# Attention products of a two-block transformer: from two ticks of the weight stream into one, in a chain

## The chip, the core and the metric

The kernel runs on one core of a Trainium2 chip. The metric is the device time of one execution in microseconds (us); lower is better. A profiled execution gives the trace from which all rows here are taken.

## The reference

Two transformer blocks run one after the other on 256 positions of width 1024, each two layers deep. Both contain softmax attention over few positions and many wide products with weights that are used once. Cut to what matters:

```python
# first block, per layer: a mixer of three branches, then SwiGLU
proj = x @ w_in                      # a_q a_k a_v | b_h b_b b_c | c_q c_k c_v | g_a g_b g_c
y_a = sliding_window_attention(a_q, a_k, a_v, sinks, slopes)   # 8 heads of 64, window 128, 2 key heads
y_b = gated_short_conv(b_h, b_b, b_c, conv_w)
y_c = moba_attention(c_q, c_k, c_v, slopes)                    # 8 heads of 64; causal over 256 here
x = layer_norm(ALPHA * x + (sigmoid(g_a) * (y_a @ w_br_a) + sigmoid(g_b) * (y_b @ w_br_b)
                            + sigmoid(g_c) * (y_c @ w_br_c)) @ w_out)
x = layer_norm(ALPHA * x + swiglu(x))
# second block, per layer, on a latent stream h and a context stream hc:
#   half a SwiGLU; then a mixer; then half a SwiGLU, all gated by products of c with w_ada
attn = attend(q_lat, [k_ctx, k_lat], [v_ctx, v_lat])           # 8 heads of 64 + 32 rotated
h = h + gt2 * merge(u @ w_bgate, conv_module, attn @ w_o_mla, fourier_mix)
#   the context stream does the same with its own keys, in the first layer only
```

## The kernel before

All weights come from memory in 765 chunks of 512 KB. ACT copies each chunk into a high part `wh`, DVE subtracts for the low part `wl` (L261), and every product of the main loops is three matmuls of high and low parts (`mm3`, through `mm`, L373). A main matmul has 256 or 512 columns.

The main loops take the weights through `wtile()` or `wchunk()`. Each time a chunk is used up they call `tick()`. A tick first takes a job of the ada products if one is due (a DMA and two DVE products named `junk`, L547), and then advances every generator in `sides` by one `next()`. What a generator emits in that step is marked to be issued after the main loop's last matmul (`issue_after(self.last_mm.ins)`); the Tile scheduler then places each instruction on its engine by its own model of when the operands are ready, so an attention product may come some way behind the tick, between main matmuls. Each engine takes its instructions in order.

Attention runs in such generators. `attn1` serves both kinds of the first block, four pairs of heads each (kind 0 the sliding window, kind 1 the other); `attn2` serves the second block in eight steps, over 256 keys for the context stream (`nk` = 1) and 512 for the latent stream (`nk` = 2). A step `s` takes two ticks. In the first tick it emits the logits of pair `s` into two banks of tag "at" and their softmax, `turn(2s - 2)` (the transposes of the first head of pair `s - 1`, three in `attn1`, `2 * nk` in `attn2`), and the values products of pair `s - 2` into the bank "pv". In the second tick it emits `turn(2s - 1)`, the second head. `turn` puts its transposes into a PSUM bank of tag "st" (there is one) and ACT copies it to `pts`.

`softmax_step` for one head is a chain over two engines: DVE adds the distance term to the logits (`z`), takes two row maxima, scales them (`nb`); ACT takes the exponentials of two parts with their sums `sm`, and of the sink (`es`); DVE adds the sink's and takes 1/sum (`rc`); ACT multiplies `z` by `rc`, first 128 columns, then 256. The transposes read that `z`. The weight splits `wh` and `wl` and the ada products stand on the same two engines.

PSUM tags: "mm" has four banks (the main loops' results), "at" two, "st", "pv" and others one (`bank`). `finish(side)` runs a generator to its end.

Of the kernel before, what the change touches and what calls it, by code (L numbers as in the profile page):

```python
# [19 lines left out]
P = 128  # L20
D = 1024
KD = D // P
T = 256
# [202 lines left out]
class Weights:  # L226


    def __init__(self, kb, dram, ahead_split, ahead_load):
        self.kb, self.dram, self.n = kb, dram, dram.shape[0]  # L230
        self.loaded = self.split = self.pos = 0
        self.raw, self.parts = {}, {}
        self.ahead_split, self.ahead_load = ahead_split, ahead_load
        self.hold = None
# [45 lines left out]
class Kernel:  # L280
    NRAW, NSPLIT, NS, NADA, CPD = 6, 5, 45, 2, 1

    def __init__(self, tc, sb, ps, aps, vec_at):
        self.tc, self.nc, self.sb, self.ps = tc, tc.nc, sb, ps
        self.aps, self.vec_at = aps, vec_at
        self.n = 0
        self.sides = []
        self.last_root = None
        self.ticks = 0
        self.ada_jobs, self.ada_next = [], 0.0  # L290
        self.cur, self.cur_i = None, 8


    def act(self, out, in_, func, bias=0.0, scale=1.0, accum_out=None):
# [46 lines left out]
    def tick(self):  # L341
        self.ticks += 1
        if self.ada_jobs and self.ticks >= self.ada_next:
            self.ada_next += self.ada_jobs[0][1]
            self.ada_jobs.pop(0)[2]()
        with self.tc.issue_after(self.last_mm.ins):
            for s in list(self.sides):
                if next(s, "end") == "end":
                    self.sides.remove(s)

    def finish(self, side):
        if side in self.sides:
            self.sides.remove(side)
        for _ in side:
            pass

    def wtile(self):
        if self.cur_i == 8:
            if self.cur is not None:
                self.tick()  # L360
            self.cur, self.cur_i = self.w.get(), 0
        i = self.cur_i
        self.cur_i += 1
        return self.cur[0][:, i, :], self.cur[1][:, i, :]
# [5 lines left out]
        return self.cur  # L370

    def mm(self, out, a, b, start, stop):
        return self.nc.tensor.matmul(out, a, b, start=start, stop=stop)  # L373

    def mm3(self, out, a, b, start, stop):
        self.mm(out, a[0], b[0], start, False)
# [547 lines left out]
    def attn1(self, kind, l, heads, q, k, v, out):  # L924

        ps, pts = {}, {}
        n = len(heads) // 2

        def turn(i):
            z = ps.pop(i)
            pt = self.bank("st", "pt").rearrange("p a b -> p (a b)")[:, :384]
            for c in range(3):
                self.nc.tensor.transpose(pt[:, c * P:(c + 1) * P], z[:, c * P:(c + 1) * P], self.ident)
            t = self.slot("pts").rearrange("p a b -> p (a b)")[:, :384]
            self.act(t, pt, AF.Copy)
            pts[i] = t

        while self.ticks % 2 != kind:  # L940
            yield
        for s in range(n + 2):
            if s < n:
                pair = heads[2 * s:2 * s + 2]
                lgs = [self.bank("at", "lg").rearrange("p a b -> p (a b)")[:, :384] for _ in pair]
                for qa, ka in (((0, P), (0, P)), ((P, T), (0, T))):
                    for (h, qt, p0, kt, *_), lg in zip(pair, lgs):
                        o = lg[:, :P] if qa[0] == 0 else lg[:, P:]
                        self.mm(o, q[qt][p0:p0 + 64, qa[0]:qa[1]], k[kt][p0:p0 + 64, ka[0]:ka[1]], True, True)
                for j in range(2):  # L950
                    ps[2 * s + j] = self.softmax_step(kind, pair[j][0], lgs[j], 384, l)
            if 0 <= s - 1 < n:
                turn(2 * s - 2)
            if 0 <= s - 2 < n:
                pair = heads[2 * s - 4:2 * s - 2]
                ts = [pts.pop(2 * s - 4 + j) for j in range(2)]
                o = self.bank("pv", "pv")[:, 0, :]
                for (*_, vc, ot, op), t in zip(pair, ts):
                    self.mm(o[op:op + 64, :], v[0][:, vc:vc + 64], t[:, :T], True, False)
                for (*_, vc, ot, op), t in zip(pair, ts):  # L960
                    self.mm(o[op:op + 64, P:], v[1][:, vc:vc + 64], t[:, 2 * P:], False, True)
                self.split_into(out[0][ot // 2][:, ot % 2, :], out[1][ot // 2][:, ot % 2, :], o)
            yield
            if 0 <= s - 1 < n:
                turn(2 * s - 1)
            yield

    def mixer1(self, l, xs, xa):
# [327 lines left out]
    def attn2(self, q, keys, vals, out, first):  # L1296


        nk = len(keys)
        scale = 96.0 ** -0.5  # L1300
        n = 8
        ps, pts = {}, {}
        pv = None

        def turn(i):
            p = ps.pop(i)
            pt = self.bank("st", "pt2").rearrange("p a b -> p (a b)")[:, :nk * T]
            for c in range(2 * nk):
                self.nc.tensor.transpose(pt[:, c * P:(c + 1) * P], p[:, c * P:(c + 1) * P], self.ident)  # L1309
            t = self.slot("pts2").rearrange("p a b -> p (a b)")[:, :nk * T]  # L1310
            self.act(t, pt, AF.Copy)
            pts[i] = t

        for s in range(n + 2):
            hp, qb = divmod(s, 2)
            while s < n and len(q) < max(hp + 1, first):
                yield
            if s < n:
                lgs = [self.bank("at", "lg2") for _ in range(2)]
                for j in range(2):  # L1320
                    qa = q[hp][0:96, j, qb * P:(qb + 1) * P]
                    for c in range(nk):
                        self.mm(lgs[j][:, c, :], qa, keys[c][hp][0:96, j, :], True, True)
                for j in range(2):
                    lf = lgs[j].rearrange("p a b -> p (a b)")[:, :nk * T]
                    mx, nb, sm, rc = self.small("mx", 1), self.small("nb", 1), self.small("sm", 1), self.small("rc", 1)
                    self.nc.vector.tensor_reduce(mx, lf, AX.X, ALU.max)
                    self.ts(nb, mx, -scale, None, ALU.mult)
                    p = self.slot("p2").rearrange("p a b -> p (a b)")[:, :nk * T]
                    self.act(p, lf, AF.Exp, bias=nb, scale=scale, accum_out=sm)  # L1330
                    self.nc.vector.reciprocal(rc, sm)
                    self.act(p, p, AF.Copy, scale=rc)
                    ps[2 * s + j] = p
            if 0 <= s - 1 < n:
                turn(2 * s - 2)
            if 0 <= s - 2 < n:
                hp, qb = divmod(s - 2, 2)
                ts = [pts.pop(2 * s - 4 + j) for j in range(2)]
                if qb == 0:
                    pv = self.bank("pv", "pv2")[:, 0, :]  # L1340
                for c in range(2 * nk):
                    for j in range(2):
                        self.mm(pv[64 * j:64 * j + 64, qb * P:(qb + 1) * P],
                                vals[c][:, 64 * (2 * hp + j):64 * (2 * hp + j) + 64],
                                ts[j][:, c * P:(c + 1) * P], c == 0, c == 2 * nk - 1)
                if qb == 1:
                    self.split_into(out[0][hp // 2][:, hp % 2, :], out[1][hp // 2][:, hp % 2, :], pv)
            yield
            if 0 <= s - 1 < n:
                turn(2 * s - 1)  # L1350
            yield

    def conv_side(self, l, ready, out):
# [443 lines left out]
```

## Time and profile before

| what | value |
|---|---|
| runs | 2925.15, 2925.62, 2922.3 us; median 2925.15 us |
| profiled execution | 2921.71 us, of which the span of its trace is 2919.9 us |
| TensorE (PE) busy | 2882.8 us, 99% of the span |
| VectorE (DVE) busy | 2060.6 us, 71% |
| ScalarE (ACT) busy | 1336.2 us, 46% |
| mean granted clock of TensorE | 0.998 of full speed |

Read it so: PE is the engine whose work makes the time; the shares of DVE and ACT are means over stages that differ. In a timeline a row gives the start, the duration, the engine, the line, and the tile written and the tiles read; PE's durations overlap, so the distance between starts is what a matmul costs. An idle time stands in brackets with what ended it.

### The profile page before, as it was taken

What the parts mean: (1) busy time and instruction counts of PE and PEld (TensorE: products, weight loads), DVE (VectorE), ACT (ScalarE), POOL (GpSimd) and SP (SyncE); (2) the same over time, 40 slices, a digit from 0 to 9 for tenths busy, and PEclk for the clock granted to TensorE, in tenths of its full rate; (3) what the DMA queues carried; (4) which work ended last, traced back from release to release, by engine and by line L of the source; (5) the groups of instructions that cost most, each with busy time, mean ns of one, the idle gap of its engine ahead of it and who ended that gap; (6) DMA issues with size and microseconds to landing.
All of it is one profiled execution on the core that took longest, in us unless ns stands there. A gap on an engine that the chain in (4) does not pass through costs nothing. (4 is left out here: it accounts for less than half of the span.)

```text
span 2919.9 us, 51534 instructions
## 1 busy us (share of the span) xinstructions
PE 2882.8 (99%) x21000; PEld 2699.4 (92%) x21000; DVE 2060.6 (71%) x3506; ACT 1336.2 (46%) x2100; POOL 109.0 (4%) x121
## 2 busy tenths in 40 slices
PE   8999999999999999999999999999999999999999
PEld 7999999899999999999999998888888888899998
DVE  7879667648657787798888785555765556877655
ACT  6645445744444432256656642222322224665444
POOL 1001001000001000010010000000100001000000
PEclk9999999999999999999999999999999999999999
DMA  7665655454555764544553453433355543435453
GB/s 271 203 224 180 219 194 164 142 181 159 201 182 166 232 223 167 171 156 144 166 178 111 152 173 131 137 130 116 110 187 166 166 159 116 162 106 170 162 182 109
DMA packets 134589, 486.66 MB, mean 167 GB/s; under 512 B 14928, under 2 KB 15184, under 8 KB 134352
## 3 DMA queue, kind: packets, MB, share of 16 engines
q1 hardware_dynamic: 133776, 482.58, 49.8%
q8 instruction: 165, 2.70, 0.4%
q10 hardware_dynamic: 576, 0.79, 0.1%
q14 instruction: 72, 0.59, 0.1%
HBM read 482.26 MB, written 1.05 MB: 166 GB/s over the span
## 5 line engine op out<-in xcount | busy, mean ns | idle before, releaser
L302 ACT ACTIVATE wh<-raw 128x1024 fp32r<-128x1024 f32 x765 | 809.5, 1059 | 1243.9 <-issue 269.9
L261 DVE TENSOR_TENSOR wl<-raw,wh 128x1024 fp32r<-128x1024 f32 x765 | 939.5, 1230 | 511.3 <-ACT wh L302 505.6
L547 DVE SCALAR_TENSOR_TENSOR junk<-ada,cb 128x1024 bf16<-128x1024 f32 x256 | 313.3, 1224 | 4.3 <-DMA ada<-in_w_ada_dram 2.2
L373 PE MATMUL f<-xh,wh 128*128 128x256 f32 x704 | 198.8, 283 | 0.0
L373 PE MATMUL f<-xh,wl 128*128 128x256 f32 x704 | 198.4, 282 | 0.0
L373 PE MATMUL f<-xl,wh 128*128 128x256 f32 x704 | 198.1, 281 | 0.0
L373 PE MATMUL g<-xh,wh 128*128 128x256 f32 x608 | 173.7, 286 | 8.8 <-ACT wh L302 7.3
L373 PE MATMUL g<-xl,wh 128*128 128x256 f32 x608 | 173.0, 285 | 0.6 <-DVE xl L308 0.6
L373 PE MATMUL g<-xh,wl 128*128 128x256 f32 x608 | 173.0, 285 | 0.0
L373 PE MATMUL bg<-wh,wh 128*128 128x256 f32 x576 | 166.8, 290 | 0.8 <-DVE q L305 0.8
L373 PE MATMUL bg<-wh,wl 128*128 128x256 f32 x576 | 163.1, 283 | 0.0
L373 PE MATMUL bg<-wl,wh 128*128 128x256 f32 x576 | 162.5, 282 | 0.0
L373 PE MATMUL b<-uh,wl 128*128 128x512 f32 (+1 forms) x384 | 145.6, 380 | 0.0
L373 PE MATMUL a<-uh,wh 128*128 128x512 f32 (+1 forms) x384 | 145.4, 380 | 0.0
L373 PE MATMUL a<-wl,wh 128*128 128x256 f32 x512 | 144.7, 283 | 0.0
L373 PE MATMUL a<-wh,wl 128*128 128x256 f32 x512 | 144.7, 283 | 0.0
L373 PE MATMUL a<-uh,wl 128*128 128x512 f32 (+1 forms) x384 | 144.1, 375 | 0.0
L373 PE MATMUL b<-ul,wh 128*128 128x512 f32 (+1 forms) x384 | 144.0, 375 | 0.0
L373 PE MATMUL a<-wh,wh 128*128 128x256 f32 x512 | 143.7, 281 | 0.0
L373 PE MATMUL a<-ul,wh 128*128 128x512 f32 (+1 forms) x384 | 143.7, 374 | 0.0
L373 PE MATMUL b<-uh,wh 128*128 128x512 f32 (+1 forms) x384 | 143.6, 374 | 0.0
L1180 POOL TENSOR_TENSOR sq<-sq,sq 128x256 f32<-128x256 f32 x63 | 64.6, 1033 | 2105.0 <-ACT sq L302 2103.6
(429 smaller groups left out, 8685.4 us busy)
## 6 DMA issues: line engine op xcount, KB each, us to landing
raw<-in_w_dram SPq DMA_DIRECT2D x765, 512.0 KB, 3.3
ada<-in_w_ada_dram SPq DMA_DIRECT2D x144, 512.0 KB, 4.1
hc<-in_ctx_dram SPq DMA_DIRECT2D x8, 256.0 KB, 4.9
x<-in_x_dram SPq DMA_DIRECT2D x4, 256.0 KB, 6.4
out_dram<-out SPq DMA_DIRECT2D x4, 256.0 KB, 2.4
cb<-in_c_dram SPq DMA_DIRECT2D x1, 512.0 KB, 8.2
cb<-in_c_ctx_dram SPq DMA_DIRECT2D x1, 512.0 KB, 8.2
dft<-in_dft_dram ACTq DMA_DIRECT2D x2, 256.0 KB, 3.3
```

The costliest lines, as they stand in the source:

```text
L261: self.last_split = kb.nc.vector.tensor_tensor(lo.rearrange("p a b -> p (a b)"), raw, f.bitcast(F32), ALU.subtract)
L302: return self.nc.scalar.activation(out, in_, func, **kw)
L373: return self.nc.tensor.matmul(out, a, b, start=start, stop=stop)
L547: self.nc.vector.scalar_tensor_tensor(junk, raw, 1.0, self.cb[:, s, :], ALU.mult, ALU.mult, accum_out=self.mods[:, l, s, c:c + 1])
L1180: self.nc.gpsimd.tensor_tensor(r["q"], r["q"], q[:, 0, :], ALU.add)
```

## The change

All products of attention that a tick emits are issued as one chain: `amm` (logits and values) and `atr` (transposes) place each behind the one before, `self.gate`. A main matmul that is emitted behind such a tick is placed behind the chain's last product (`mm` with `behind`). The gate is reset at every tick. The second head's `turn` moves from the second tick into the first, behind the first head's, and the second tick emits no products. The transposes' banks come from "mm" in place of "st".

```diff
@@ tick
+        self.gate, self.in_side = None, True
         with self.tc.issue_after(self.last_mm.ins):
             for s in list(self.sides):
                 if next(s, "end") == "end":
                     self.sides.remove(s)
+        self.in_side = False
@@ mm and new functions
     def mm(self, out, a, b, start, stop):
-        return self.nc.tensor.matmul(out, a, b, start=start, stop=stop)
+        with self.behind(not self.in_side):
+            return self.nc.tensor.matmul(out, a, b, start=start, stop=stop)
+    def behind(self, on):
+        return self.tc.issue_after(self.gate.ins) if on and self.gate is not None else contextlib.nullcontext()
+    def amm(self, out, a, b, start, stop):
+        with self.behind(True):
+            self.gate = self.nc.tensor.matmul(out, a, b, start=start, stop=stop)
+    def atr(self, out, a):
+        with self.behind(True):
+            self.gate = self.nc.tensor.transpose(out, a, self.ident)
@@ attn1 (attn2 in the same way)
         def turn(i):
             z = ps.pop(i)
-            pt = self.bank("st", "pt").rearrange("p a b -> p (a b)")[:, :384]
+            pt = self.bank("mm", "pt").rearrange("p a b -> p (a b)")[:, :384]
             for c in range(3):
-                self.nc.tensor.transpose(pt[:, c * P:(c + 1) * P], z[:, c * P:(c + 1) * P], self.ident)
+                self.atr(pt[:, c * P:(c + 1) * P], z[:, c * P:(c + 1) * P])
...
             if 0 <= s - 1 < n:
                 turn(2 * s - 2)
+                turn(2 * s - 1)
...
             yield
-            if 0 <= s - 1 < n:
-                turn(2 * s - 1)
             yield
```

The first place is the second step of the sliding-window side in layer 0, behind main matmul 240, near 40 us in the trace. `lg` are logits, `pt` transposes, `z_406` and `z_424` the two heads of the first pair, `g_47` a main product. PE before; between the two pieces 36 main matmuls on `g_47`:

```order
246 L373 MATMUL lg_505<-qk_381,qk_383 128x128
247 L373 MATMUL lg_506<-qk_381,qk_383 128x128
248 L373 MATMUL lg_505<-qk_381,qk_383 128x256
249 L373 MATMUL lg_506<-qk_381,qk_383 128x256
250 L935 MATMUL pt_547<-ident,z_406 128x128 x3
...
286 L373 MATMUL g_47_504<-xh_105,wl_445 128x256
287 L935 MATMUL pt_589<-ident,z_424 128x128
288 L373 MATMUL g_47_504<-xh_109,wh_444 128x256
289 L373 MATMUL g_47_504<-xl_110,wh_444 128x256
290 L935 MATMUL pt_589<-ident,z_424 128x128 x2
```

PE now:

```order
246 L388 MATMUL lg_505<-qk_381,qk_383 128x128
247 L388 MATMUL lg_506<-qk_381,qk_383 128x128
248 L388 MATMUL lg_505<-qk_381,qk_383 128x256
249 L388 MATMUL lg_506<-qk_381,qk_383 128x256
250 L392 MATMUL pt_547<-ident,z_406 128x128 x3
251 L392 MATMUL pt_553<-ident,z_424 128x128 x3
252 L379 MATMUL g_47_504<-xh_101,wh_353 128x256
253 L379 MATMUL g_47_504<-xl_102,wh_353 128x256
```

The transposes of the second head have moved up over 36 main matmuls and are no longer cut in two.

ACT at the same place, before; `pts` is the copy of a head's transposes, `es` the sink's exponential, `wh` a weight copy:

```order
35 L302 ACTIVATE es_436<-nb_427,vecs 128x2
36 L302 ACTIVATE pts_551<-pt_547 128x384
37 L302 ACTIVATE wh_685<-raw_595 128x1024
38 L302 ACTIVATE z_424<-z_424,rc_429 128x128
39 L302 ACTIVATE z_424<-z_424,rc_429 128x256
40 L302 ACTIVATE pts_593<-pt_589 128x384
```

ACT now:

```order
35 L303 ACTIVATE es_436<-nb_427,vecs 128x2
36 L303 ACTIVATE pts_551<-pt_547 128x384
37 L303 ACTIVATE z_424<-z_424,rc_429 128x128
38 L303 ACTIVATE z_424<-z_424,rc_429 128x256
39 L303 ACTIVATE pts_557<-pt_553 128x384
```

The weight copy no longer stands ahead of the two copies that finish `z_424`. On DVE the sequence there is the same in both kernels but for line numbers and buffers; now:

```order
37 L309 SCALAR_TENSOR_TENSOR z_529<-dist,lg_506 128x384
38 L261 TENSOR_TENSOR wl_562<-raw_472,wh_561 128x1024
39 L306 TENSOR_TENSOR sm_428<-sm_428,es_436 128x2
40 L566 SCALAR_TENSOR_TENSOR junk_0_0_591,mods<-ada_0_589,cb 128x1024
41 L938 RECIPROCAL rc_429<-sm_428 128x2
```

The reciprocal of the second head stands behind the first ada product, as it did before.

The second place is the fourth step of the same side, behind main matmul 336. PE before (`pv` are values products, `cv` a main product):

```order
362 L373 MATMUL lg_760<-qk_381,qk_385 128x256
363 L935 MATMUL pt_713<-ident,z_529 128x128
364 L373 MATMUL pv_807<-pts_674,va_390 64x256
365 L935 MATMUL pt_713<-ident,z_529 128x128 x2
366 L373 MATMUL cv_751<-wh_597,xh_101 128x512
367 L373 MATMUL cv_751<-wl_598,xh_101 128x512
368 L373 MATMUL cv_751<-wh_597,xl_102 128x512
369 L373 MATMUL cv_752<-wh_597,xh_101 128x512
370 L373 MATMUL cv_752<-wl_598,xh_101 128x512
371 L373 MATMUL pv_807<-pts_717,va_390 64x256
372 L373 MATMUL pv_807<-pts_674,va_390 64x128
373 L373 MATMUL pv_807<-pts_717,va_390 64x128
```

PE now:

```order
361 L388 MATMUL lg_760<-qk_381,qk_385 128x256
362 L392 MATMUL pt_801<-ident,z_634 128x128 x3
363 L392 MATMUL pt_807<-ident,z_652 128x128 x3
364 L388 MATMUL pv_813<-pts_674,va_390 64x256
365 L388 MATMUL pv_813<-pts_680,va_390 64x256
366 L388 MATMUL pv_813<-pts_674,va_390 64x128
367 L388 MATMUL pv_813<-pts_680,va_390 64x128
368 L379 MATMUL cv_751<-wh_597,xh_101 128x512
```

The values products of a pair stand in one piece, behind both heads' transposes of the next pair; before, five main matmuls stood in their middle. Over the whole kernel PE's main matmuls are interrupted at 109 places before and at 55 now, each now at a chunk's end, with the same number of matmuls.

## Rows read from the trace of the kernel before

**Rows 1.** The page, busy us, share of the span and instructions by engine.

```profile
PE 2882.8 (99%) x21000; PEld 2699.4 (92%) x21000; DVE 2060.6 (71%) x3506; ACT 1336.2 (46%) x2100; POOL 109.0 (4%) x121
```

**Rows 2.** PE's waits: line and tile, releaser; us in total, times, longest.

```profile
PE bg L373 <- DVE q L305: 0.8, 1, 0.8
PE pt L1309 <- ACT pts L302: 0.8, 1, 0.8
PE pt L935 <- ACT z L302: 0.7, 2, 0.5
```

**Rows 3.** Windows: us; busy PE, PEld, DVE, ACT, POOL; PEclk, DMA share, GB/s.

```profile
32.40:78.10 45.70, 44.99 (x308) 36.34 (x307) 37.99 (x91) 33.95 (x86) 0.00 (x0) 1.00 0.61 200
```

**Rows 4.** Timeline of PE, layer 0: start and duration in us, engine, line.

```profile
74.06 0.28 PE L373 MATMUL b<-xh,wl 128*128 128x256 f32 x1
...
75.06 0.28 PE L373 MATMUL b<-xl,wh 128*128 128x256 f32 x1
...
76.34 0.28 PE L373 MATMUL b<-xh,wh 128*128 128x256 f32 x1
76.61 0.86 PE L373 MATMUL pv<-pts,va 128*64 128x256 f32 x6
...
77.62 0.28 PE L373 MATMUL b<-xh,wl 128*128 128x256 f32 x1
...
97.38 0.28 PE L373 MATMUL b<-xh,wl 128*128 128x256 f32 x1
97.50 0.49 PE L935 MATMUL pt<-ident,z 128*128 128x128 f32 x3
...
97.95 0.28 PE L373 MATMUL b<-xl,wh 128*128 128x256 f32 x1
...
117.73 0.27 PE L373 MATMUL b<-xh,wl 128*128 128x256 f32 x1
117.94 0.87 PE L373 MATMUL pv<-pts,vc 128*64 128x256 f32 x8
...
118.96 0.28 PE L373 MATMUL b<-xl,wh 128*128 128x256 f32 x1
```

**Rows 5.** Timeline of PE behind main matmul 240.

```profile
40.45 0.55 PE L935 MATMUL pt<-ident,z 128*128 128x128 f32 x3
40.75 0.37 PE L373 MATMUL g<-xh,wh 128*128 128x256 f32 x1
```

**Rows 6.** Timeline of DVE there.

```profile
42.76 1.22 DVE L547 SCALAR_TENSOR_TENSOR junk<-ada,cb 128x1024 bf16<-128x1024 f32 x1
...
43.90 0.16 DVE L919 RECIPROCAL rc<-sm 128x2 f32<-128x2 f32 x1
```

**Rows 7.** Timeline of ACT there.

```profile
43.79 1.06 ACT L302 ACTIVATE wh<-raw 128x1024 fp32r<-128x1024 f32 x1 [1.02 <-PE g L373]
44.76 0.79 ACT L302 ACTIVATE z<-z,rc 128x128 f32<-128x128 f32 x2
```

**Rows 8.** Timeline of PE and DVE, the same place of layer 1.

```profile
504.90 0.55 PE L935 MATMUL pt<-ident,z 128*128 128x128 f32 x3
508.35 0.16 DVE L919 RECIPROCAL rc<-sm 128x2 f32<-128x2 f32 x1
```

**Rows 9.** Timeline of PE and ACT, last pair of the side, layer 0.

```profile
67.27 0.38 PE L935 MATMUL pt<-ident,z 128*128 128x128 f32 x2
71.04 0.78 ACT L302 ACTIVATE z<-z,rc 128x128 f32<-128x128 f32 x2
```

**Rows 10.** Windows, columns as in the third group: around two idle times of PE.

```profile
469.20:472.60 3.40, 1.48 (x11) 1.06 (x9) 3.20 (x7) 2.12 (x4) 0.00 (x0) 0.99 0.49 154
472.60:475.80 3.20, 3.02 (x14) 3.02 (x15) 3.17 (x10) 1.02 (x2) 1.57 (x3) 0.50 0.52 164
936.90:941.00 4.10, 1.80 (x16) 1.62 (x15) 2.97 (x6) 2.20 (x4) 2.80 (x5) 1.00 0.24 82
941.00:944.40 3.40, 3.40 (x30) 3.40 (x30) 3.27 (x8) 1.33 (x2) 0.00 (x0) 1.00 0.57 202
```

More of the change, by code (lines that the diff above doesn't have):

```diff
@@ L291, in __init__ @@
         self.cur, self.cur_i = None, 8
+        self.in_side, self.gate = False, None
     def act(self, out, in_, func, bias=0.0, scale=1.0, accum_out=None):
@@ L353, in finish @@
             self.sides.remove(side)
+        self.in_side = True
         for _ in side:
             pass
+        self.in_side = False
     def wtile(self):
@@ L948, in attn1 @@
                         o = lg[:, :P] if qa[0] == 0 else lg[:, P:]
-                        self.mm(o, q[qt][p0:p0 + 64, qa[0]:qa[1]], k[kt][p0:p0 + 64, ka[0]:ka[1]], True, True)
+                        self.amm(o, q[qt][p0:p0 + 64, qa[0]:qa[1]], k[kt][p0:p0 + 64, ka[0]:ka[1]], True, True)
                 for j in range(2):
@@ L958, in attn1 @@
                 for (*_, vc, ot, op), t in zip(pair, ts):
-                    self.mm(o[op:op + 64, :], v[0][:, vc:vc + 64], t[:, :T], True, False)
+                    self.amm(o[op:op + 64, :], v[0][:, vc:vc + 64], t[:, :T], True, False)
                 for (*_, vc, ot, op), t in zip(pair, ts):
-                    self.mm(o[op:op + 64, P:], v[1][:, vc:vc + 64], t[:, 2 * P:], False, True)
+                    self.amm(o[op:op + 64, P:], v[1][:, vc:vc + 64], t[:, 2 * P:], False, True)
                 self.split_into(out[0][ot // 2][:, ot % 2, :], out[1][ot // 2][:, ot % 2, :], o)
             yield
-            if 0 <= s - 1 < n:
-                turn(2 * s - 1)
             yield
@@ L1306, in turn @@
             p = ps.pop(i)
-            pt = self.bank("st", "pt2").rearrange("p a b -> p (a b)")[:, :nk * T]
+            pt = self.bank("mm", "pt2").rearrange("p a b -> p (a b)")[:, :nk * T]
             for c in range(2 * nk):
-                self.nc.tensor.transpose(pt[:, c * P:(c + 1) * P], p[:, c * P:(c + 1) * P], self.ident)
+                self.atr(pt[:, c * P:(c + 1) * P], p[:, c * P:(c + 1) * P])
             t = self.slot("pts2").rearrange("p a b -> p (a b)")[:, :nk * T]
@@ L1322, in attn2 @@
                     for c in range(nk):
-                        self.mm(lgs[j][:, c, :], qa, keys[c][hp][0:96, j, :], True, True)
+                        self.amm(lgs[j][:, c, :], qa, keys[c][hp][0:96, j, :], True, True)
                 for j in range(2):
@@ L1335, in attn2 @@
                 turn(2 * s - 2)
+                turn(2 * s - 1)
             if 0 <= s - 2 < n:
@@ L1342, in attn2 @@
                     for j in range(2):
-                        self.mm(pv[64 * j:64 * j + 64, qb * P:(qb + 1) * P],
+                        self.amm(pv[64 * j:64 * j + 64, qb * P:(qb + 1) * P],
                                 vals[c][:, 64 * (2 * hp + j):64 * (2 * hp + j) + 64],
@@ L1348, in attn2 @@
             yield
-            if 0 <= s - 1 < n:
-                turn(2 * s - 1)
             yield
```

## The prediction

> **What bounds the kernel now.** I read the page first. TensorE (PE) is busy for 2882.8 of 2919.9 us, VectorE (DVE) for 71% and ScalarE (ACT) for 46% [rows 1]. The other 37 us of PE are start, end and a few chains between layers; so the time is the sum of PE's steps, and whatever puts a step or a wait into PE's queue is paid in full, while DVE and ACT have room on the average. I then asked what PE waits for. Of that list the attention sides hold only three entries, 0.8, 0.8 and 0.7 us [rows 2], 2.3 us together and about 2.6 with waits too short to be listed. So before the change the attention products hardly wait: they are issued where their operands are there already. In the stretch of layer 0's first attention (32.4 to 78.1 us) PE is busy 44.99 of 45.70 us at a granted clock of 1.00, and DVE 37.99 and ACT 33.95 [rows 3]: here the two helpers are at 83% and 74%, far above their averages. What is worth asking is therefore what an interruption of the main stream costs, and when the operands are ready at the places where the products now stand.
>
> **What an interruption costs.** I count from the start of the last main matmul ahead of the attention products to the start of the second one behind them, less two steps of 0.12 us. Three transposes alone: 97.38 to 97.95, so 0.57 - 0.24 = 0.33 us, 0.11 each [rows 4]. Inside a longer string a transpose also takes 0.11 or less (three starts between 40.45 and 40.75, [rows 5]). So joining a string of transposes to another string saves nothing by itself; there is no entry fee. The values products do differ. A whole pair (two of 128x256, two of 128x128): 117.73 to 118.96, 1.23 - 0.24 = 0.99 us. A pair with main matmuls in its middle: 0.76 (74.06 to 75.06) plus 1.04 (76.34 to 77.62) = 1.80 us [rows 4]. A broken pair costs 0.8 us more.
>
> **Gains.** Six pairs of values stand broken before (three in the sliding-window side of layer 0, two and one in the other kind of layers 0 and 1): 6 x 0.8 = 4.8 us. In the latent stream of layer 1 some logits and values are cut by other products: about 1.5, by the same counting. Transposes cut into one and two: 1.0 over all. The waits of [rows 2] with the short ones: 2.6. Sum 9.9 us. Laid over all places, the attention products take 131.1 us of PE before and 121.2 if none waits. This is what the change can give.
>
> **The moved transposes and what they wait for.** The second head of a pair is turned one tick earlier. Its transposes need z after ACT's two copies with 1/sum (rc), and the pair's softmax stands serially on DVE and ACT behind the weight splits and the ada products, whose order on DVE the change leaves as it is. I laid the new order out with the durations of the old trace; two places carry the result.
>
> Place one, the second tick of the sliding-window side, layer 0 (main matmul 240). PE has the first head's three transposes started by 40.75 [rows 5]. The second head's rc stands on DVE behind the first ada product: that runs 42.76 to 43.98, rc 43.90 to 44.06 [rows 6]. Nothing ahead of it there depends on PE's main stream, so it can't come earlier. Before, ACT did a weight copy of 1.06 us at 43.79, then the two z copies at 44.76 [rows 7]; in the new order the z copies go first, so they start at 44.06 and the first ends at 44.06 + 0.40 = 44.46. PE stands from 40.75 to 44.46: 3.7 us, and 0.3 more because the second and third transposes need the second copy (0.40 against 0.11). Total 4.0. Everything main is queued behind these transposes on PE, so no other work hides it: before, 36 main matmuls stood there. In layer 1 rc comes at 508.35, and the first head's transposes at 504.90 [rows 8], behind two weight splits in place of an ada product: again 508.51 + 0.40 - (504.90 + 0.30) = 3.7, plus 0.3. Two places: 8.0 us.
>
> Place two, the last pair of the same side (main matmul 360 in layer 0, and its like in layer 1). Before, the first head's last two transposes start at 67.27 and the second head's copies at 71.04, 71.44 at the earliest for a transpose [rows 9]: 4.1 us apart. In the new order the tick itself comes later (an earlier wait has moved it, while DVE and ACT ran on), and with the remaining steps (exponentials, sum, rc, a weight copy, z copy) 2.4 us stay, plus 0.3. Both layers: 5.4.
>
> By the same laying out: third tick's pair of layer 0, 1.3; the last pair of the other kind in layer 0, 1.7 (its values wait for ACT's copy of the second head's transposes); seven ticks with 0.2 to 0.6 each, 1.7; latent stream of layer 0, 1.3 for a transpose and 0.9 for a gate product; of layer 1, 1.7 and 1.6. The gate products wait because transposes now sit in two of the four banks of the main loop; the nearest row is the 0.8 that a gate product waits now [rows 2]. In the context stream none waits. Sum of waits: 8.0 + 5.4 + 1.3 + 1.7 + 1.7 + 2.2 + 3.3 = 23.6 us.
>
> Bounds. None of these waits is in the trace of before. The lower end is half of them, 11.8, if DVE and ACT, which PE's standing gives time, get ahead more than I laid out; the upper end is 23.6 plus 5 if the shared banks also hold up main products elsewhere (some six ticks at the 0.8 of [rows 2]). I take 23.6, since at the two large places each step has its row.
>
> **The clock.** Where PE idles the granted clock can fall. In the stretch from 472.6 to 475.8, after PE was busy for 1.48 of 3.4 us, it is 0.50, that is 1.2 in place of 2.4 GHz; 14 matmuls start there in 3.20 us. At 1.00, 30 start in 3.40 us [rows 10]. So one such fall costs 3.20 - 14 x 3.40/30 = 1.6, say 1.7 us with its edges. But after PE was busy for 1.80 of 4.10 us at 936.9 it stayed at 1.00 [rows 10]. Between these I give the two waits of 4 us, longer than any of these, a fall each: 3.4 us, and none to those of 2.4. Bounds: none (0) to all waits above 2 us plus the latent ones (five, 8.5).
>
> On this the Trainium skill has a rule ("TensorE: Matmul & The Clock Gate", "Loop structure matters more than you think"): matmuls stay at full clock where dense strings follow one another, and run slow where a long wait stands between them. The trace bears it out at 472 and not at 937, so the sum by the rule would be 8.5 in place of 3.4 us, which is the upper bound already taken.
>
> **Cost at nothing.** Chaining alone (products wait for the previous one on the same in-order engine), the unchanged number of matmuls, logits at their old ticks, and the queues of SP and POOL, past which nothing is moved.
>
> **Sum.** -9.9 + 23.6 + 3.4 = +17.1 us. The profiled execution took 2921.7 (span 2919.9 and 1.8 around it), so 2938.8 on its basis; the median of the runs is 2925.15, 3.4 above, and I carry the difference over: 2942.
>
> **Rivals.** (a) Only the joining is seen: the softmax of the second head is ready. This decides itself on whether the second z copy ends before the first head's third transpose. For: at some forty of the 55 places I find no wait. Against: 3.7 us at both large places, with rows for each step. 2925.15 - 9.9 = 2915, faster. (b) The waits come out at half: 2925.15 - 9.9 + 11.8 = 2927, no change; it would need DVE to have rc done some 2 us earlier at [rows 6], where the ada product stands ahead. (c) More falls of the clock and main products held up by the banks: 17.1 + (8.5 - 3.4) + 5 = +27, so 2952; partly so, 2947. For: the stretch of [rows 3] leaves the helpers little room, and every wait there delays the weight splits' release. Against: 937. (d) The strings of transposes bring the clock down without any wait. If each of the 40 ticks with transposes cost a fall of 1.7 us, that is 68 us, about 3006. Against it: strings of logits and three transposes stand in the stretch of [rows 3] at 1.00. Its ground is a rule of the Trainium skill ("TensorE: Matmul & The Clock Gate", "Part 4: PE-mode transpose"): transposes don't count as busy time in the way of products; no run here shows that. (e) The change doesn't do what it says: the order shows 109 interruptions before and 55 now, each at a chunk's end, so I give this nothing.
>
> **Chances.** Forecast 0.71, (a) 0.04, (b) 0.08, (c) 0.15, (d) 0.02. From no change a measurement tells about 0.2%, 5.9 us: faster is below 2919.3, slower above 2931.0. Faster 0.04, within 0.08, slower 0.88. The range has to leave out no more than 2 in 10: from 2930 (waits two thirds as large, no fall of the clock: -9.9 + 15.7 = +5.8) to 2952 (case c in full).
>
> **What would show it.** In the profile after: a PE wait for ACT's z of 3 to 4 us near 41 us and again near 505, and of about 2.4 near 68 and 530 to 540; in the list of waits the transposes of z at 15 to 18 us in place of 0.7; no values product split by main matmuls; a granted clock of 0.5 for some 3 us behind the two long waits. Wrong would be the forecast if the transposes' waits add up to less than 10 us, which points to (a) or (b); a total above 2950 with many waits of main products for banks points to (c).

## The result, and the profile after

The changed kernel is slower: 2949.99 us (median; 2948.55 to 2950.76) against 2924.17 us of the kernel before, a ratio of 1.009 with a 95% interval from 1.008 to 1.0101. That is 25.8 us. The spans of the two profiled executions, 2919.9 and 2948.1 us, lie 28.2 us apart; the profiled execution of the kernel before took 2921.71 us, 2.5 less than its median.

The page of the changed kernel says that PE is busy some 11 us longer and stands for the rest; the work on DVE and ACT is the same but for 3 us (against [rows 1]):

```profile
PE 2893.4 (98%) x21000; PEld 2708.7 (92%) x21000; DVE 2061.9 (70%) x3506; ACT 1338.8 (45%) x2100; POOL 107.9 (4%) x121
```

PE's waits of the changed kernel, the entries that answer to [rows 2] (line and tile, releaser; us in total, times, longest):

```profile
PE pt L392 <- ACT z L303: 15.1, 9, 3.6
...
PE bg L379 <- DVE q L306: 1.8, 2, 1.0
...
PE pt L392 <- DVE ffl L306: 1.4, 1, 1.4
...
PE pt L392 <- DVE q L306: 1.1, 1, 1.1
```

Transposes that wait for `z` went from 0.7 to 15.1 us. In all, the attention strings (attention products that follow each other without a main product between) wait 20.5 us, where they waited 2.6. Of the 20.5, 4.8 us stand at two places of the latent stream, where transposes and the gate product (the first main product behind a chain, `bg`) wait, but for 0.3 us, for DVE's `ffl` and `q` and not for a softmax.

This is the first of the two large places, the tick behind main matmul 240, in the timelines of PE, ACT and DVE (to be held against [rows 5 to 7]):

```profile
39.82 0.93 PE L388 MATMUL lg<-qk,qk 64*128 64x128 f32 x8
40.68 0.55 PE L392 MATMUL pt<-ident,z 128*128 128x128 f32 x3
...
44.85 1.08 PE L392 MATMUL pt<-ident,z 128*128 128x128 f32 x3 [3.62 <-ACT z L303]
45.58 0.56 PE L379 MATMUL g<-xh,wh 128*128 128x256 f32 x1
45.94 0.41 PE L379 MATMUL g<-xl,wh 128*128 128x256 f32 x1
46.16 0.41 PE L379 MATMUL g<-xh,wl 128*128 128x256 f32 x1
```

```profile
42.53 0.47 ACT L303 ACTIVATE pts<-pt 128x384 f32<-128x384 f32 x1
44.39 0.80 ACT L303 ACTIVATE z<-z,rc 128x128 f32<-128x128 f32 x2 [1.40 <-DVE rc L938]
```

```profile
41.78 1.22 DVE L261 TENSOR_TENSOR wl<-raw,wh 128x1024 fp32r<-128x1024 f32 x1
42.92 0.16 DVE L306 TENSOR_TENSOR sm<-sm,es 128x2 f32<-128x2 f32 x1
42.99 1.22 DVE L566 SCALAR_TENSOR_TENSOR junk<-ada,cb 128x1024 bf16<-128x1024 f32 x1
...
44.13 0.16 DVE L938 RECIPROCAL rc<-sm 128x2 f32<-128x2 f32 x1
```

Read it backwards. The second head's three transposes start at 44.85, 3.62 us after PE ran dry. They wait for ACT's copies of `z` (44.39), these for DVE's `rc` (44.13), and that stands on DVE behind an ada product of 1.22 us, although its sum was there at 43.08. The weight copy that stood ahead of ACT's copies before is gone, as the order had it. The main matmuls behind show the second loss: they start 0.22 us apart (45.94, 46.16) where a step costs 0.12. The clock has fallen.

The windows behind the long waits (us; busy PE, PEld, DVE, ACT, POOL; PEclk, DMA share, GB/s):

```profile
46.00:50.00 4.00, 4.00 (x21) 4.00 (x21) 2.35 (x8) 1.63 (x6) 0.00 (x0) 0.50 0.68 204
...
77.00:81.00 4.00, 4.00 (x19) 3.22 (x18) 0.62 (x2) 1.16 (x2) 0.00 (x0) 1.00 0.34 128
...
521.00:525.00 4.00, 4.00 (x21) 4.00 (x21) 1.56 (x8) 2.77 (x11) 0.00 (x0) 0.52 0.36 114
...
550.80:554.50 3.70, 3.70 (x14) 2.94 (x14) 0.42 (x1) 0.30 (x2) 0.00 (x0) 0.81 0.23 85
...
1580.00:1583.50 3.50, 3.50 (x19) 3.50 (x20) 3.46 (x9) 1.50 (x3) 0.00 (x0) 0.57 0.09 15
...
2582.50:2586.50 4.00, 4.00 (x19) 4.00 (x20) 3.91 (x10) 0.78 (x2) 0.00 (x0) 0.50 0.00 0
```

Behind five of the six places where a string waits more than 2 us the granted clock is at half for a part of the window or for all of it; behind one (77 to 81) it stays at 1.00, and the 19 matmuls there are fewer because they have 512 columns. At the first four places the wait is a single one of 2.2 or 3.6 us. At the two of the latent stream it is 2.4 us in several waits, none above 1.4.

**Where the 28.2 us went.** I take the same measure as in the prediction, the start of the last main matmul ahead to the start of the second one behind less two main steps, over all attention strings: 131.1 us before, 151.0 after, so 19.9 more. That holds +17.9 of listed waits (2.6 to 20.5), about +4.4 where the transposes wait for the second of the two `z` copies (ten places, 0.44 each; overlapping ends hide these from the list of waits), about +3 of slow clock inside the strings, and a remainder of -5.4, which is what joining gives. The slow main matmuls behind the five places cost 2.2, 2.0, 0.9, 1.5 and 1.9 us, +8.5. Together 28.4. The hidden waits and the price of the clock are estimates from the distances between starts.

### The profile page after: what moved, and what is told of

Read it like the earlier page. It is cut to its first block, busy times and chain, and to the rows that moved or that the text cites. A ratio compares the mean times of both kernels' runs of the same rounds, so it can differ in the third digit from the quotient of the medians.

```text
span 2948.1 us, 51555 instructions
## 1 busy us (share of the span) xinstructions
PE 2893.4 (98%) x21000; PEld 2708.7 (92%) x21000; DVE 2061.9 (70%) x3506; ACT 1338.8 (45%) x2100; POOL 107.9 (4%) x121
```

## The experiments

The theory: the second head's transposes, moved up one tick, wait for their softmax; PE's idling there brings the clock down; chain, gate and banks cost nothing of size. The rivals: the chain and the gate cost; the transposes in main banks cost; long strings, not waits, bring the clock down.

### The second head back in the second tick

```diff
@@ attn1 and attn2, from the changed kernel
                 turn(2 * s - 2)
-                turn(2 * s - 1)
...
             yield
+            if 0 <= s - 1 < n:
+                turn(2 * s - 1)
             yield
```

> The changed kernel with one part undone: the second head's transposes go back to the second tick; the chain, the gate for main products and the banks of the main loop stay. Theory (the moved transposes wait for their softmax, and the long waits bring the clock down): the waits of 3.6 us near 41 and 515 us fall to about 1.5, no wait is above 2 us, the clock falls after attention waits are gone (mean granted clock 0.998), time 2922 to 2928. Rival one (the chain and the gate themselves cost, or the shared banks hold up main products): most of the 26 us stays, above 2938.

2926.86 us, ratio to the kernel before 1.0011 (1.0002 to 1.0019). 23 of the 26 us are gone with this one part, chain, gate and banks all kept. What is left of the transposes' waits for `z`, and the waits of the latent stream for DVE, from the list of waits of this kernel:

```profile
PE pt L392 <- ACT z L303: 4.1, 3, 1.4
...
PE bg L379 <- DVE ffl L306: 1.4, 1, 1.4
...
PE pt L392 <- DVE q L306: 1.1, 1, 1.1
```

The clock stays up at 45 and 509 us. One fall behind an attention wait is left, which I had not expected: near 2558 us, behind the 1.1 us of the last line, the granted clock is 0.50 from 2558.4 to 2561.8. So the move of the second head is the cause of most of the loss. The rival that chain, gate and banks make it by themselves falls: without the move they are within some 3 us of the kernel before, with an interval that begins just above no change (1.0002).

### The same with the bank st

```diff
@@ turn in attn1 and attn2, from e1_back
-            pt = self.bank("mm", ...)
+            pt = self.bank("st", ...)
```

> As e1_back, but the transposes go into the single bank st again, as in the kernel before. Theory: with one bank the transposes of one tick wait for ACT to empty those of the tick before, and with the gate main products stand behind them; so transposes' waits grow by 10 to 20 us against e1_back, 2935 to 2945, with falls of the clock where a wait passes 3 us. Rival (transposes in main banks hold up the main products): faster than e1_back by the gate product's wait of 1 to 2 us, no more waits.

2944.22 us, ratio 1.0071 (1.0058 to 1.0083): 17 us more than with the main loop's banks. The list of waits:

```profile
PE pt L392 <- ACT pts L303: 14.8, 9, 5.3
PE pt L392 <- ACT z L303: 4.1, 3, 1.4
```

Waits for ACT's copy out of the one bank, up to 5.3 us, take the place. The two waits of e1_back for `ffl` and `q` (1.4 and 1.1 us) are gone, so the main banks have a price of some 2.5 us of waits there. The single bank costs far more: with a gate, a transpose that waits for its bank holds up the main products too. Two falls of the clock stand behind shorter waits than the 3 us that I had expected them from: near 70 and 107 us, behind 1.4 and 2.0 us.

### Both heads in the second tick; everything in the first tick but one pair later

```diff
@@ e3_both_second: attn1 and attn2, from the changed kernel
-            if 0 <= s - 1 < n:
-                turn(2 * s - 2)
-                turn(2 * s - 1)
...
             yield
+            if 0 <= s - 1 < n:
+                turn(2 * s - 2)
+                turn(2 * s - 1)
             yield
@@ e6_late: attn1 and attn2, from the changed kernel; values of pair s - 3, n + 3 steps
-            if 0 <= s - 1 < n:
-                turn(2 * s - 2)
-                turn(2 * s - 1)
+            if 0 <= s - 2 < n:
+                turn(2 * s - 4)
+                turn(2 * s - 3)
```

> The changed kernel with both heads' transposes together in the second tick, and logits and values in the first. Strings of six or eight transposes stay as they are. Theory: the second head's softmax has one tick more, its waits shrink to about 1.2 us at the two large places, no falls of the clock in layer 0 and 1 sides, 2921 to 2928. Rival (strings of transposes, not waits, bring the clock down): the falls stay near 45, 520, 1580 and 2583 us, mean granted clock near 0.993, above 2932.

> The changed kernel with everything in one chain in the first tick, but a pair's transposes one pair later and its values two pairs after that (one more step at a side's end). The chain at a tick is as long as in the changed kernel. Theory: transposes of z wait 3 us at one place (the last pair of the first side) and hardly elsewhere, at most one fall of the clock, 2918 to 2925. Rival (length of the chain or the gate costs): as the changed kernel but for the waits' own 20 us, falls of the clock remain, above 2930.

Both are the kernel before within what can be told: 2925.57 us (1.0006; 0.9997 to 1.0015) and 2923.73 us (1.0001; 0.9993 to 1.001). The second one keeps the long strings of the changed kernel: in each latent stream's side logits, eight transposes and values stand in one chain, main products gated, five times in a row (six in the changed kernel), and in the first block six transposes follow each other everywhere. Its windows, first over most of the latent stream's side of layer 0, then over the first steps of layer 0's first side:

```profile
1563.00:1632.00 69.00, 69.00 (x586) 65.06 (x586) 55.23 (x118) 48.72 (x90) 0.00 (x0) 1.00 0.36 123
32.40:53.50 21.10, 21.10 (x177) 19.66 (x175) 19.13 (x45) 15.97 (x39) 0.00 (x0) 1.00 0.67 228
```

PE without a gap, the clock at 1.00. So strings do not bring the clock down. What remains there is a wait of 2.8 us of the last pair of the first side, with a fall of the clock behind it that costs some 1.7 us, and one of 1.1 us of a gate product in layer 1's latent stream, with a second fall (0.50 from 2556.4 to 2559.8), where I had allowed for one at most. The expected lower ends (2918 and 2921) were too low: I had left these two out or taken them too small. In e3_both_second values products wait 4.0 us at one place of layer 0 for ACT's copy of the transposes, with the clock at 0.50 from 104 to 108 us behind; I had expected neither. The joining itself can be read here: the attention strings of e6_late take 128.4 us, of which 5.1 are listed waits and by estimate 1.5 the hidden ones and the slow clock: 121.8 against 128.5 of the kernel before without its waits.

### Main products free

```diff
@@ mm, from the changed kernel
-        with self.behind(not self.in_side):
-            return self.nc.tensor.matmul(out, a, b, start=start, stop=stop)
+        return self.nc.tensor.matmul(out, a, b, start=start, stop=stop)
```

> The changed kernel without the gate on main products: the chain within a tick and both heads' turns in the first tick stay, but main products may be placed between the chain's links. Theory: the two large waits stay where the scheduler still puts the second head's first transpose behind the first head's (3.4 us each at 41 and 515 us), those of the last pairs go; attention waits 10 to 14 us in place of 20.5, falls of the clock at 4 places, 2935 to 2943. Rival (the gate makes the whole loss): 2922 to 2928.

2940.7 us, 1.006 (1.0048 to 1.0073), inside the theory's range, with attention waits of some 14 us, at the upper end of those expected, and the clock down behind attention waits at the four places expected. At both large places the scheduler still puts the first of the second head's transposes right behind the first head's, and it waits 3.6 us there with the whole queue behind it; the waits of the last pairs are gone (`z` 9.4 us in all in place of 15.1). Without the gate 9 of the 26 us are gone and 17 stay: the gate makes part of the loss, the place of the transposes most of it.

### Without the two copies by 1/sum

```diff
@@ softmax_step, from the changed kernel
-        self.act(z[:, :P], z[:, :P], AF.Copy, scale=rc[:, 0:1])
-        self.act(z[:, P:], z[:, P:], AF.Copy, scale=rc[:, 1:2])
```

> The changed kernel without the two copies that multiply z by 1/sum in the first block (left out, so the first block's attention is not normalised there and DVE's 1/sum is used by nobody); the order of PE is the same. Theory: the second head's z is ready some 2.8 us earlier, the two large waits fall from 3.6 to about 0.7, the last pair's to about 1, the falls of the clock near 45, 520 and 550 us vanish, and the waits of the second block and their falls stay: 2930 to 2936. Rival (the waits come from something else than the softmax chain, such as the banks): above 2943.

2931.93 us (2928.88 to 2933.55), 1.0027 (1.0016 to 1.0037), as forecast. With the order of PE the same but for eight of its 21000 matmuls, the waits in the first block's strings shrink from 15.1 us to this:

```profile
PE pt L392 <- ACT z L303: 5.1, 12, 1.3
```

At the first large place the wait is now 0.9, and the clock behind it stays at 1.00:

```profile
43.40:47.40 4.00, 4.00 (x36) 4.00 (x35) 4.00 (x11) 1.27 (x2) 0.00 (x0) 1.00 0.42 140
```

The second block still has both its places with 2.4 us of waits and both falls of the clock. So the first block's waits are the softmax chain's length, and the clock there goes with the waits. Those of the second block are of another kind, for DVE and the main banks.

### PE kept busy in the two long waits

```diff
@@ attn1, from the changed kernel: e7_pad_mm; e8_pad_tr has 32 times atr(du[:, :P], q[0][:, :P])
                 turn(2 * s - 2)
+                if kind == 0 and s == 1:
+                    du = self.bank("st", "du")[:, 0, :]
+                    for _ in range(14):
+                        self.amm(du, q[0][:, :P], q[0], True, True)
                 turn(2 * s - 1)
```

> The changed kernel with 14 idle products (128 rows by 256 columns, float32, into an unused bank, result not used) between the two heads' transposes at the two large waits (41 and 515 us), so that PE works where it waited. Theory: the transposes there wait at most 1 us, the granted clock stays at 1.00 behind them, the falls of about 2 us each near 45 and 520 go while the time of the wait itself stays: 2944 to 2948, 2 to 5 us below the changed kernel. Rival (the clock falls for another reason than PE's idling): falls stay and the time is that of the changed kernel or more.

> As e7_pad_mm, with 32 idle transposes of 128x128 in place of the products (3.5 us by 0.11 each). If a string of transposes keeps the clock as products do: no fall near 45 and 520, 2944 to 2948. If transposes don't count as work for the clock: falls of about 2 us stay at both places, 2948 to 2952.

With transposes as filling, the timeline of PE at the first place, and the windows behind both:

```profile
40.25 0.55 PE L392 MATMUL pt<-ident,z 128*128 128x128 f32 x3
40.63 3.66 PE L392 MATMUL du<-ident,qk 128*128 128x128 f32 x32
44.42 0.84 PE L392 MATMUL pt<-ident,z 128*128 128x128 f32 x3
```

```profile
45.50:49.50 4.00, 4.00 (x35) 4.00 (x35) 2.69 (x11) 2.88 (x9) 0.00 (x0) 1.00 0.65 196
...
519.50:523.50 4.00, 4.00 (x36) 4.00 (x35) 1.56 (x8) 3.77 (x13) 0.00 (x0) 1.00 0.41 132
```

The second head's transposes start where they did, since their softmax is no sooner done; but the clock behind is 1.00 at both places, and 35 matmuls start in 4 us where 21 did. 2945.67 us, 4.3 below the changed kernel, while PE does 64 transposes more. With products as filling the clock stays at 1.00 at both places too, but the 14 took 6.2 us in place of the 3.4 that I had meant them to take, so that the first place costs 1.6 us more than the wait; and 2952.42 us is outside what I expected. The totals hold another shift. In both kernels the third pair's transposes, some 20 us on in layer 0, wait 3.6 us in place of 0.9, with a slow stretch behind that costs 1.0 us with transposes and 1.9 with products as filling, and layer 0's last pair's wait of 2.2 is gone: the order on DVE came out differently there. With transposes as filling the clock also stays at 1.00 behind the 2.2 us wait of layer 1's last pair, from 541 to 551 us, where nothing was filled and where it fell in the changed kernel. The clock's part is therefore read from the windows, not from the totals.

That a string of transposes holds the clock as well as products do differs from the rule that (d) in the prediction weighed (the Trainium skill, "TensorE: Matmul & The Clock Gate", "Part 4: PE-mode transpose"): after 3.66 us of transposes and nothing else the clock is 1.00. The measurement decides, for what it covers: such a string keeps the clock up that stood at 1.00 ahead of it. Whether it raises a low clock no run here tests, and the trace, which records these transposes as MATMUL with `ident`, does not show whether they run in the page's transpose mode.

### The changed kernel once more, and the best of the parts

> The changed kernel as it is, one more profiled execution. If the clock falls by the wait alone, falls stand again behind all five waits (near 45, 520, 550, 1580 and 2583 us) and not near 75. If it is partly chance for waits of 2.2 to 2.4 us, the two waits of 3.6 us have their falls again and one or more of the others differs.

2949.15 us. All five falls stand again at the same places, and again none behind the 2.2 us wait at 72 us:

```profile
46.00:50.00 4.00, 4.00 (x22) 4.00 (x22) 2.19 (x7) 1.47 (x6) 0.00 (x0) 0.55 0.73 235
...
77.00:81.00 4.00, 4.00 (x19) 3.22 (x18) 0.75 (x2) 1.06 (x1) 0.00 (x0) 1.00 0.26 100
...
521.00:525.00 4.00, 4.00 (x24) 4.00 (x23) 1.56 (x8) 2.86 (x12) 0.00 (x0) 0.62 0.32 115
545.50:550.80 5.30, 3.23 (x13) 1.91 (x14) 1.83 (x4) 3.22 (x9) 0.00 (x0) 0.73 0.57 182
...
1580.00:1583.50 3.50, 3.50 (x23) 3.50 (x23) 3.49 (x9) 1.50 (x3) 0.00 (x0) 0.69 0.14 42
...
2582.50:2586.50 4.00, 4.00 (x23) 4.00 (x23) 3.54 (x9) 0.81 (x3) 0.00 (x0) 0.60 0.00 0
```

So chance between executions is not a likely reason for that one wait to leave the clock up, though two executions are too few to exclude it.

> The best of the parts: the first block's attention as in the kernel before (bank st, second head in the second tick, no chain), the second block's as in e6_late (chained, both heads' transposes one pair later, banks of the main loop). Theory: the first block's new waits are gone with it (about 4 us and a fall of the clock against e6_late), its broken values are back (5 us); the second block keeps the 2 us of its joined products. 2920 to 2924, at the edge of what can be told from the kernel before. Rival (late chained products cost in the second block): above 2926.

The first block's `attn1` is that of the kernel before, the second block's `attn2` that of e6_late. 2922.23 us, 0.9994 (0.9985 to 1.0003): inside the range, and not to be told from the kernel before. No version here beats it measurably.

## Why the prediction was right, point by point

The direction and the range held: 2942 forecast with 2930 to 2952, 2950.0 measured. The forecast moved by 17 us, the kernel by 26, and by 28 between the profiled executions; most of the difference sits in one term, the clock. That the time lies inside the range is in part luck: its upper edge held 5 us for main products that the banks hold up elsewhere, which did not come, and 8.5 for the clock, where by the account above some 11.5 came.

- **What bounds the kernel.** Right: PE's steps and waits add up to the change in the span, while the work of DVE and ACT is the same but for 3 us.
- **Joining gives 9.9 us.** About right. The waits of 2.6 us went as counted. The rest I had at 7.3: e6_late, where hardly anything waits, shows 6.7, and the changed kernel leaves 5.4 as a remainder of its account.
- **The two large places, 8.0 us.** Right in every step. [rows 6] gave the ada product ahead of `rc`, [rows 7] the copies: 3.62 us of listed wait and about 0.45 hidden against 3.7 and 0.3. e5_no_norm shows that the chain behind `rc` is what is waited for, e1_back that it is the tick which makes it a wait.
- **The last pairs, 5.4 us.** 2.2 listed and 0.44 hidden at each: 5.3.
- **The sum of waits, 23.6 us.** 20.5 listed and 4.4 hidden: 24.9, near enough. The half that (b) reckoned with was wrong.
- **Main banks.** I had the gate products wait for them, 2.5 us in all; they wait 1.8. In the latent stream transposes also wait for a main bank (1.4 and 1.1 us, released by DVE), which I had in part. Both kinds stand at places where the clock also fell. Held against the single bank (e2_back_st, 14.8 us), this was the cheaper side.
- **The clock, 3.4 us.** This term was mis-sized: I gave falls to the two waits of 4 us and none to those near 2.4, by the window at 936.9 [rows 10]. There were five falls, the three others behind one wait of 2.2 us and two groups of shorter ones of 2.4 us each, for 8.5 us behind the strings and about 3 inside them. The upper bound of that step (five falls, 8.5) had the number right and the price low, since part of a fall lies in the string itself, ahead of the main matmuls that I had counted. With 11.5 in place of 3.4 the sum is 25.2. What misled me is the one row at 936.9, taken as a sign that such waits leave the clock up: for the same wait it is 0.71 behind in e1_back (942.4 to 945.8) and 0.50 in e6_late.
- **The rule on loop structure** that the prediction weighed (the Trainium skill, "TensorE: Matmul & The Clock Gate", "Loop structure matters more than you think") was the better guide here: at five of the six places with more than 2 us of waiting between dense strings the clock fell, and filling the two longest waits kept it up.
- **The rivals.** (a) needs the softmax done in time; at nine waits it was not. (c) came true in its clock part alone. (d) is refuted by e6_late and e8_pad_tr. To (e): one of the 55 interruptions is still the second piece of a cut chain. In layer 0's other kind three main matmuls on `b` stand behind the fourth of six transposes, between 119 and 122 us; nothing of the sum hangs on it.

What stays open is why one wait of 2.2 us (layer 0, 72 us) leaves the clock at 1.00 and its like of layer 1 (2.2 us, 545 us) doesn't, in both executions of the changed kernel. In e8_pad_tr that of layer 1 leaves it at 1.00 too, so the length of the wait alone does not decide it.

## What to carry to other kernels

Before several small products on an in-order engine are put together, lay out when the operands of the last of them are ready: the string starts its tail no sooner than the slowest chain behind it, and everything in the queue waits along. Joining pays only where a group was cut in two (0.8 us a pair here); a move by one tick earlier cost 23 us (against e1_back), and a move later cost nothing that could be told (e6_late). Waits on the matrix engine should be priced with the clock: here five falls cost some 11.5 us, some 2 to 3 each, on top of 2.2 to 3.6 us of waiting a place, and whether a wait brings one is not certain.

## What the runs showed of the hardware

The length of the last wait alone does not tell whether the granted clock falls: in e1_back it was at half behind one of 1.1 us near 2558 us, with one of 0.3 ahead of it, and in the changed kernel it stayed at 1.00 behind one of 2.2 us at 73 us. For one wait it is not the same in all kernels: behind 2.3 us of waiting for `sq` near 938 us it stayed at 1.00 in the kernel before [rows 10], and was at half in e6_late for the same products:

```profile
937.80:941.90 4.10, 1.79 (x16) 1.61 (x15) 2.97 (x7) 2.20 (x4) 2.92 (x5) 1.00 0.27 79
941.90:945.10 3.20, 3.20 (x16) 3.20 (x17) 2.31 (x6) 1.08 (x2) 0.00 (x0) 0.50 0.54 175
```

Two kernels can thus differ at a place where their work is the same, in this window by some 1.4 us (3.20 less 16 matmuls at the 3.40/30 of [rows 10]). And 32 transposes in 3.66 us, with nothing else on PE, kept the clock at full.
